# Latent attention: the row maxima written in rounded form, the rows of sums behind the last values, and in two of eight units the last low part behind the maxima

## The chip, the cores and the metric

The kernel runs on one core of one Trainium2 chip. Its time is the device time of one execution, in microseconds (us). The core has five engines: TensorE (PE in the profile; PEld are its weight loads), VectorE (DVE), ScalarE (ACT), GpSimd (POOL) and SyncE (SP), which issues most of the DMAs.

## What is computed

Two layers of a diffusion backbone for 128 context tokens and 1024 latent tokens. The change lies in layer 0, in the attention of the 1024 latent tokens over 128 cached and 1024 own keys, for 16 heads:

```python
s = (jnp.einsum('bqhd,bkhd->bhqk', q_nope, k_nope)
     + jnp.einsum('bqhr,bkr->bhqk', q_rope, k_rope)) * MLA_SCALE
p = softmax_f32(s).astype(v.dtype)
return jnp.einsum('bhqk,bkhd->bqhd', p, v)
...
return (o.reshape(b, n, MLA_WIDTH) * jax.nn.silu(gate)) @ w_out
```

A softmax may have any number taken off all scores of one query before the exponential, as long as it is the same number in the numerator and in the sum.

## The kernel before

Most products are made to keep float32's precision out of fp32r operands: a value is split into a rounded high part and a low part (the rest), and a product takes three passes, high by high, high by low, low by high. So each exponential of six of the nine key blocks is split: ACT writes the high part, DVE subtracts it for the low part.

The attention is a loop over 64 **units**: unit k is head k // 4 and query block k % 4 (256 queries). Nine blocks of 128 keys fill five PSUM banks (three named S, two named T) with transposed scores: keys on partitions, queries in columns. While unit k is worked on (`un`), the scores of the next one (`nx`) are made. The order of the steps on PE, ACT, DVE and POOL is written out by hand, in a table `ORDERS` with one row for each k % 8 (called the **kind** of a unit below). Each engine executes its instructions in that order and waits where an operand is not there. The steps that matter here:

- `s0`..`s4` (PE): scores of the next unit, a bank each. Bank S of `s0` is free again when `e0` of the present unit has read it.
- `m0`..`m4`: running maximum of the scores; `m0` a copy on ACT, the others on DVE.
- `e0`..`e4` (ACT): exponentials, a bank each. `h0`..`h2` (ACT) and `l0`..`l2` (DVE): their high and low parts.
- `+1`..`+4` (POOL): sums of the exponentials over the key blocks, five operations that each need the one before.
- `v68`, `v03`, `v45` (PE): values of key blocks 6 to 8 (six matmuls in the profile's groups), 0 to 3 (twelve) and 4 and 5 (six).
- **Sums**: `L0` (PE) turns the sums into columns, `L1` (DVE) reduces them to one number for each query and inverts it, `L2` and `L3` (DVE) split it into high and low part (`lir`), `L4` (PE) makes it a row again, `L5` (ACT) copies the row into `row`.
- **Maxima of the next unit**: `M0` (PE) turns them into columns, `M1` (DVE) reduces them (`nm`), `M2` and `M3` (DVE) split them (`nmr`), `M4` (PE) makes them a row, `M5` (ACT) copies the row into two rows of the queries' tile `q`, and `X` (PE, nine matmuls) adds them to all scores. Only then can the next unit's `e0` begin.
- `V` (ACT): the values out of PSUM (`ol`). `F` (PE, `finish`): the row of inverted sums on all partitions, and the last product of the values. `O` (DVE): the gating.
- The other letters (`P`, `p`, `A`, `ES`, `EV`, `H`, `T`, `w`) place work of the next heads: projections, rope, prompt attention, weight splits.

`L0`, `M0`, `M4` and `L4` write the same PSUM bank, `pm`. Steps that the diff's functions don't show:

```python
def columns_to_rows(r, ps):
    for k in range(2):
        nc.tensor.matmul(ps[:, k * P:(k + 1) * P], r[:, 2 * k:2 * k + 2], identR, start=True, stop=True)
def max_rows_out(un):
    S.copy(un["ql"][64:66, un["qs"]], un["pm"][0:2, 256:512])
def sum_row_out(un):
    S.copy(row[0:2, :], un["rs"][0:2, 0:256])
```

Of the kernel before, what the change touches and what calls it, by code (L numbers as in the profile page):

```python
# [11 lines left out]
F32 = mybir.dt.float32  # L12
F32R = mybir.dt.float32r
AF = mybir.ActivationFunctionType
ALU = mybir.AluOpType
AX = mybir.AxisListType
# [3 lines left out]
P = 128  # L20
# [7 lines left out]
H = 16  # L28
# [5 lines left out]
EPS = 1e-6  # L34
GW = 64
ORDERS = [
# [8 lines left out]
]  # L45
NPF = 5
WHOLE = 6
# [10 lines left out]
def hybrid_step(ctx: ExitStack, tc: tile.TileContext, i, o):  # L58
    nc = tc.nc
    V, S, G = nc.vector, nc.scalar, nc.gpsimd  # L60
# [705 lines left out]
    def max_cols(un, pm):  # L766
        un["pm"] = pm
        for k in range(2):
            nc.tensor.transpose(pm[:, k * P:(k + 1) * P], un["rm"][:, k * P:(k + 1) * P], ident)

    def max_reduce(un):
        un["nm"] = p2a.tile([P, 2], F32, tag="nm2", name="nm2", bufs=2)
        V.tensor_reduce(un["nm"], un["pm"][:, 0:256].rearrange("p (a b) -> p a b", a=2), AX.X, ALU.max, negate=True)

    def part_hi(un, src, name):
        un[name] = r = p2a.tile([P, 4], F32R, tag=name, name=name, bufs=2)
        V.tensor_copy(r[:, 0::2], un[src])

    def part_lo(un, src, name):
        r = un[name]  # L780
        V.tensor_tensor(r[:, 1::2], un[src], r[:, 0::2].bitcast(F32), ALU.subtract)
# [98 lines left out]
    def new_unit(h, u):  # L880
        hp = hps[h]
        return dict(h=h, qs=slice(u * 256, u * 256 + 256), qA=hp["qA"], qh=hp["q2"][0], ql=hp["q2"][1], wv=head_wv[h],
                    banks=[], pf=[], pT=[])


    p2a = es_a.enter_context(tc.tile_pool(name="p2a", bufs=1, side="right", reuse_waits="tile"))
    q2_, qA_ = [[p2a.tile([P, NTOK], F32R, name=f"q2{x}_{n}") for x in range(2)] for n in range(2)], [
        [p2a.tile([P, NTOK], F32R, name=f"qA{x}_0") for x in range(2)]]

    def no_max(q2):  # L890

        G.memset(q2[1][64:66, NLAT:NTOK].bitcast(F32), 0.0)
    for q2 in q2_:
        no_max(q2)
# [13 lines left out]
    f, un, nx = None, None, new_unit(0, 0)  # L908
    with tc.high_priority(offset=300):
        for b in range(5):  # L910
            scores(nx, b)
            run_max(nx, b)
        max_cols(nx, bank("W"))
        max_reduce(nx)
        part_hi(nx, "nm", "nmr")
        part_lo(nx, "nm", "nmr")
        max_rows(nx)
        max_rows_out(nx)
        last_scores(nx)
# [22 lines left out]
    def do(fn, x, *a):  # L942
        if x:
            fn(x, *a)
# [61 lines left out]
    for k, (h, u) in enumerate(units):  # L1006
        if k + 1 < len(units):

            hn, n = units[k + 1]
            do_rest((hn, (0, 1, 1, 2)[n]))  # L1010
        if u == 3 and h < H - 1 or (h, u) == (H - 1, 0):
            first, *rest = prompt_work(h)
            heads.appendleft(first)
            prompts.extend(rest)
            if h + 2 < H:
                heads.extend(head_work(h + 2))
        if u == 1 and h % 2 == 1 and h < H - 1:
            while prompts:
                do_rest(1)
        splits = deque()  # L1020
        if u == 1 and h + 1 < H:
            if h:
                splits.append(lambda: load_v(h + 1))
            splits.append(lambda: h + 2 < H and head_raw.update({h + 2: load_head(h + 2, new_raw(0))}))
        if u == 2 and h + 2 < H:
            splits.append(lambda: split_qk(h + 2, head_raw[h + 2][0]))
            splits.append(lambda: split_r(h + 2, head_raw[h + 2][1]))
        f, un, nx = un, nx, new_unit(*units[k + 1]) if k + 1 < len(units) else None
        pm = None
        if k == len(units) - 2:  # L1030
            early_load()
        last = k == len(units) - 1
        for step in ORDERS[k % 8].split():
            if last and step in ("h0", "L0"):
                early_product((0, 1) if step == "h0" else (2,))
                n = "h0 L0".split().index(step)
                early_split(2 * n, (q2_[(H - 2) % 3], qA_[(H - 1) % 2])[n])
                load_half(2 * n + 4, new_raw())
            c, n = step[0], int(step[1:] or 0) if step[1:].isdigit() else step[1:]
            if c == "e":  # L1040
                exp(un, n)
            elif c == "F":
                do(finish, f)
            elif c == "O":
                do(finish_out, f)
            elif c == "E":
                do_evac({"V": V, "S": S}[n])
            elif c == "h":
                hi(un, n)
            elif c == "l":  # L1050
                lo(un, n)
            elif c == "s":
                do(scores, nx, n)
            elif c == "m":
                do(run_max, nx, n)
            elif c in "Pp":
                do_prod(c == "p")
            elif c == "H":
                if splits:
                    splits.popleft()()  # L1060
            elif c == "w":
                if 36 <= k < 44:
                    load_wo0(k - 36)
            elif c == "+":
                sums(un, n)
            elif c == "v":
                n = step[1:]
                values(un, range(int(n[0]), int(n[-1]) + 1))
            elif c == "M":
                if n == 0:  # L1070
                    pm = pm if pm is not None else bank("M")
                    do(max_cols, nx, pm)
                elif n == 1:
                    do(max_reduce, nx)
                elif n == 2:
                    do(part_hi, nx, "nm", "nmr")
                elif n == 3:
                    do(part_lo, nx, "nm", "nmr")
                elif n == 4:
                    do(max_rows, nx)  # L1080
                elif n == 5:
                    do(max_rows_out, nx)
            elif c == "L":
                if n == 0:
                    pm = pm if pm is not None else bank("M")
                    sum_cols(un, pm)
                elif n == 1:
                    sum_inverse(un)
                elif n == 2:
                    part_hi(un, "li", "lir")  # L1090
                elif n == 3:
                    part_lo(un, "li", "lir")
                elif n == 4:
                    sum_rows(un)
                elif n == 5:
                    sum_row_out(un)
            elif c == "A":
                do_after(1)
            elif c == "T":
                settle()  # L1100
            elif c == "V":
                values_out(un)
            elif c == "X":
                do(last_scores, nx)
            else:
                assert False, step
# [48 lines left out]
    for t in range(NT):  # L1155
        ps = bank("S")[:, :256] if t else early["ps"]
        for q in range(4) if t else ():
            n = 4 * (t - 1) + q
# [109 lines left out]
    for t in range(NT):  # L1268
# [4 lines left out]
        for q in range(4):  # L1273
            n = 32 + 4 * t + q
# [510 lines left out]
    for k in range(-2, N):  # L1785
# [15 lines left out]
        if k >= 0 and (its[k]["cg"], its[k]["e"]) == (0, 0):  # L1801
            p = its[k]["p"]
# [5 lines left out]
        for step in NORDER.split():  # L1808
            c, n = step[0], step[1:]
# [159 lines left out]
```

## Time and profile before

| | |
|---|---|
| median of 3 runs | 2148.03 us (2146.34 to 2150.01) |
| the profiled execution | 2152.5 us, its span from first to last instruction 2150.7 us |
| busy: PE / DVE / ACT / POOL | 94% / 64% / 49% / 38% of the span |
| mean granted TensorE clock | 0.982 of full speed |

Busy shares are means over the whole program. The attention loop runs from about 354 to 1175 us of the span. A "unit" below is about 12 to 14 us long.

### The profile page before, as it was taken

What the parts mean: (1) busy time and instruction counts of PE and PEld (TensorE: products, weight loads), DVE (VectorE), ACT (ScalarE), POOL (GpSimd) and SP (SyncE); (2) the same over time, 40 slices, a digit from 0 to 9 for tenths busy, and PEclk for the clock granted to TensorE, in tenths of its full rate; (3) what the DMA queues carried; (4) which work ended last, traced back from release to release, by engine and by line L of the source; (5) the groups of instructions that cost most, each with busy time, mean ns of one, the idle gap of its engine ahead of it and who ended that gap; (6) DMA issues with size and microseconds to landing.
All of it is one profiled execution on the core that took longest, in us unless ns stands there. A gap on an engine that the chain in (4) does not pass through costs nothing. (4 is left out here: it accounts for less than half of the span.)

```text
span 2150.7 us, 36948 instructions
## 1 busy us (share of the span) xinstructions
PE 2027.4 (94%) x12894; PEld 1857.6 (86%) x12894; DVE 1371.6 (64%) x3032; ACT 1057.4 (49%) x2430; POOL 821.9 (38%) x820
## 2 busy tenths in 40 slices
PE   8899998899999999999998799989999999999898
PEld 3899997888888898888898788889889999999686
DVE  4723886667777777786776735542215788888743
ACT  5645115455555565555554533342215666667631
POOL 1411213566766667776764500010001333333300
PEclk9999999999999999999999999999999999999899
DMA  8212753112221213221212733325424655556753
GB/s 296 92 69 91 241 172 84 51 53 61 57 70 45 68 53 84 61 76 35 75 31 84 232 128 124 117 87 180 151 97 145 187 171 179 176 183 199 217 150 97
DMA packets 177230, 256.44 MB, mean 119 GB/s; under 512 B 20946, under 2 KB 142578, under 8 KB 177044
## 3 DMA queue, kind: packets, MB, share of 16 engines
q1 hardware_dynamic: 176780, 253.71, 38.2%
q8 instruction: 102, 1.67, 0.3%
q14 instruction: 84, 0.69, 0.1%
q10 hardware_dynamic: 136, 0.26, 0.0%
q0 software_dynamic: 128, 0.11, 0.0%
HBM read 182.58 MB, written 51.49 MB: 109 GB/s over the span
## 5 line engine op out<-in xcount | busy, mean ns | idle before, releaser
L826 POOL TENSOR_TENSOR sm<-sm,pf 128x512 f32<-128x512 f32 (+1 forms) x192 | 260.6, 1357 | 17.9 <-ACT pf L805 4.0
L815 DVE TENSOR_TENSOR pT<-pf,pT 128x512 fp32r<-128x512 f32 x192 | 231.2, 1212 | 40.5 <-ACT pT L810 40.2
L88 PE MATMUL ps_W<-h,w 128*128 128x384 f32 x1152 | 237.6, 345 | 0.4 <-DVE w L83 0.4
L747 PE MATMUL ps_S<-qA,cKT 128*128 128x256 f32 x1152 | 202.8, 296 | 4.1 <-ACT pf L805 3.9
L88 PEld LDWEIGHTS ps_W<-h,w 128*128 128x128 f32 x1152 | 197.9, 188 | 6.4 <-DVE w L83 0.8
L88 PE MATMUL ps_S<-hT,w_hi 128*128 128x384 f32 x720 | 193.0, 347 | 4.3 <-DVE hT L83 2.6
L747 PEld LDWEIGHTS ps_S<-qA,cKT 128*128 128x128 f32 x1152 | 171.8, 193 | 10.6 <-ACT pf L805 6.3
L88 PE MATMUL ps_M<-pT,cK 128*128 128x256 f32 x1152 | 168.1, 290 | 0.0
L1655 POOL TENSOR_SCALAR pf<-pf,li 128x512 f32<-128x512 f32 x128 | 91.2, 712 | 198.5 <-DVE li L1652 180.2
L88 PEld LDWEIGHTS ps_M<-pT,cK 128*128 128x128 f32 x1152 | 146.5, 190 | 0.0
L88 PEld LDWEIGHTS ps_S<-hT,w_hi 128*128 128x128 f32 x720 | 133.8, 193 | 6.1 <-DVE hT L83 3.3
L823 POOL TENSOR_TENSOR sm<-pf 128x512 f32<-128x512 f32 x64 | 86.6, 1354 | 115.4 <-ACT pf L805 114.9
L88 PE MATMUL ps_S<-wo,og 128*128 128x512 f32 x432 | 124.9, 397 | 0.0
L88 PE MATMUL ps_S<-hT,w_lo 128*128 128x384 f32 x360 | 123.9, 345 | 0.0
L521 ACT COPY qt<-ps_W 128x384 f32<-128x384 f32 (+1 forms) x104 | 46.6, 448 | 149.6 <-PE ps_W L88 136.3
L810 ACT CAST pT<-pf 128x512 fp32r<-128x512 f32 x192 | 118.9, 631 | 0.0
L1649 ACT ACTIVATE pf<-pf,nm 128x512 f32<-128x512 f32 x128 | 93.0, 726 | 34.5 <-DVE nm L1646 30.9
L747 PE MATMUL ps_S<-q,KR 128*128 128x256 f32 x384 | 109.1, 285 | 0.4 <-DMA q<-w_raw 0.4
L805 ACT ACTIVATE pf<-ps_S 128x512 f32<-128x512 f32 x192 | 108.0, 597 | 0.2 <-PE ps_S L798 0.2
L747 PE MATMUL ps_T<-qA,cKT 128*128 128x256 f32 x576 | 101.7, 292 | 0.0
L792 ACT CAST q<-ps_M 2x256 fp32r<-2x256 f32 x63 | 22.8, 361 | 160.2 <-PE ps_M L786 160.1
L83 DVE TENSOR_TENSOR og<-w_raw,og 128x512 fp32r<-128x512 f32 x56 | 54.6, 994 | 70.0 <-ACT og L149 69.9
(379 smaller groups left out, 5133.3 us busy)
## 6 DMA issues: line engine op xcount, KB each, us to landing
w_raw<-in_w_ada SPq DMA_DIRECT2D x48, 512.0 KB
w_raw<-og_d SPq DMA_DIRECT2D x41, 512.0 KB
vw<-vd SPq DMA_DIRECT2D x128, 128.0 KB
bias<-in_bias SPq DMA_DIRECT2D x64, 192.0 KB
q<-rp SPq DMA_DIRECT2D x126, 96.0 KB
gate_d<-gt SPq DMA_DIRECT2D x48, 192.0 KB
w_raw<-in_wgate SPq DMA_DIRECT2D x16, 512.0 KB
gt<-gate_d SPq DMA_DIRECT2D x64, 128.0 KB
```

Source lines behind the costliest of these rows:

```text
L83: eng.tensor_tensor(out, a, b, ALU.subtract)
L88: nc.tensor.matmul(ps, lhs[a], rhs[b], start=first and n == 0, stop=last and n == 2)
L521: (eng.copy if eng is S else eng.tensor_copy)(out, src)
L747: nc.tensor.matmul(ps[:, c:c + 256], k_[:, j, :], q_[:, un["qs"]], start=c == 0 and n == 0, stop=n == 3, skip_group_check=True)
L792: S.copy(un["ql"][64:66, un["qs"]], un["pm"][0:2, 256:512])
L805: S.activation(pf, un["banks"][b][:, :w], AF.Exp)
L810: S.copy(un["pT"][b][0][:, :pf.shape[1]], pf)
L815: V.tensor_tensor(x[1], pf, x[0].bitcast(F32), ALU.subtract)
L823: G.tensor_tensor(un["sm"], un["pf"][0], pf, ALU.add)
L826: G.tensor_tensor(sm[:, :w], sm[:, :w], pf, ALU.add)
L1649: S.activation(it["pf", rg], it["pf", rg], AF.Exp, bias=it["nm", rg], scale=1.0, accum_out=it["li", rg])
L1655: G.tensor_scalar(it["pf", rg], it["pf", rg], it["li", rg][:, 0:1], 1.0, ALU.mult, ALU.mult)
```

## The change

Three things. The maxima are written by `M1` in rounded form (fp32r) at once, into one of two tiles of four columns whose low columns were set to zero at the start, so `M2` and `M3` are gone: every score of a query is lowered by the rounded maximum. In all eight rows of the table `L4` and `L5` stand behind `v45`, and `M4`, `M5` right before it. In the rows of kinds 5 and 6 `l2` stands behind `m4`. The diff, with two of the eight table rows:

```diff
-    "F e0 H O ES s0 H e1 +1 h0 s1 l0 T e2 A m0 e3 m1 e4 s2 P m2 T h1 +2 +3 s3 l1 h2 l2 m3 P +4 p s4 m4 v68 ES p L0 M0 L1 M1 L2 v03 p A M2 L3 ES M3 w L4 M4 v45 A M5 L5 X V",
+    "F e0 H O ES s0 H e1 +1 h0 s1 l0 T e2 A m0 e3 m1 e4 s2 P m2 T h1 +2 +3 s3 l1 h2 m3 P +4 p s4 m4 l2 v68 ES p L0 M0 L1 M1 L2 v03 p A L3 ES w M4 M5 v45 L4 L5 A X V",
-    "H F e0 H e1 s0 T O +1 h0 s1 l0 e2 A m0 m1 h1 e3 s2 +2 P P +3 s3 l1 m2 h2 l2 e4 ES m3 v68 s4 +4 A m4 p L0 M0 L1 P M1 A A L2 M2 A v03 P L3 M3 ES L4 A M4 w v45 M5 X L5 V ES",
+    "H F e0 H e1 s0 T O +1 h0 s1 l0 e2 A m0 m1 h1 e3 s2 +2 P P +3 s3 l1 m2 h2 l2 e4 ES m3 v68 s4 +4 A m4 p L0 M0 L1 P M1 A A L2 A v03 P L3 ES A M4 M5 w v45 L4 L5 X V ES",
...
     def max_reduce(un):
-        un["nm"] = p2a.tile([P, 2], F32, tag="nm2", name="nm2", bufs=2)
-        V.tensor_reduce(un["nm"], un["pm"][:, 0:256].rearrange("p (a b) -> p a b", a=2), AX.X, ALU.max, negate=True)
+        un["nmr"] = nmr_[un["h"] * 4 + un["qs"].start // 256 & 1]
+        V.tensor_reduce(un["nmr"][:, 0::2], un["pm"][:, 0:256].rearrange("p (a b) -> p a b", a=2), AX.X, ALU.max,
+                        negate=True)
...
+    nmr_ = [p2a.tile([P, 4], F32R, name=f"nmr{x}") for x in range(2)]
+    for x in nmr_:
+        G.memset(x.bitcast(F32), 0.0)
...
         max_reduce(nx)
-        part_hi(nx, "nm", "nmr")
-        part_lo(nx, "nm", "nmr")
...
-                elif n == 2:
-                    do(part_hi, nx, "nm", "nmr")
-                elif n == 3:
-                    do(part_lo, nx, "nm", "nmr")
```

What this makes of the engines' order is shown at three places. First PE at the end of unit 28 (kind 4), as in most units: the last matmuls of `v03`, the rows, `v45` (six matmuls `ps_M<-pT`), and `X` (`ps_S<-q,KR`). Before:

```order
L88 MATMUL ps_M<-pT_8090,cK_864 128x256
L786 MATMUL ps_M<-identR,lir 2x128 x2
L786 MATMUL ps_M<-identR,nmr 2x128 x2
L88 MATMUL ps_M<-pT_8095,cK_863 128x256
L88 MATMUL ps_M<-pT_8096,cK_863 128x256
L88 MATMUL ps_M<-pT_8095,cK_864 128x256
L88 MATMUL ps_M<-pT_8095,cK_863 128x256
L88 MATMUL ps_M<-pT_8096,cK_863 128x256
L88 MATMUL ps_M<-pT_8095,cK_864 128x256
L798 MATMUL ps_S<-q_1_2873,KR_867 128x256 x6
```

and with the change:

```order
L88 MATMUL ps_M<-pT_7978,cK_864 128x256
L788 MATMUL ps_M<-identR,nmr_2877 2x128 x2
L88 MATMUL ps_M<-pT_7983,cK_863 128x256
L88 MATMUL ps_M<-pT_7984,cK_863 128x256
L88 MATMUL ps_M<-pT_7983,cK_864 128x256
L88 MATMUL ps_M<-pT_7983,cK_863 128x256
L88 MATMUL ps_M<-pT_7984,cK_863 128x256
L88 MATMUL ps_M<-pT_7983,cK_864 128x256
L788 MATMUL ps_M<-identR,lir 2x128 x2
L800 MATMUL ps_S<-q_1_2873,KR_867 128x256 x6
```

The row of sums (`lir`) moved from ahead of the row of maxima (`nmr`) to between `v45` and `X`; nothing else on PE moved. Second, ACT at the same place, with the engines whose semaphores each row waits for: `M5`, `L5`, `V` and the next unit's first two exponentials. Before:

```order
L792 CAST q_1_2873<-ps_M 2x256 [waits DVE_49,PE_49]
L860 CAST row<-ps_M 2x256
L843 COPY ol<-ps_M 128x256 [waits PE_49]
L805 ACTIVATE pf<-ps_S 128x512 [waits PE_49,Pool_49]
L805 ACTIVATE pf<-ps_S 128x512 [waits PE_49]
```

and with the change:

```order
L794 CAST q_1_2873<-ps_M 2x256 [waits DVE_49,PE_49]
L862 CAST row<-ps_M 2x256 [waits PE_49]
L845 COPY ol<-ps_M 128x256
L807 ACTIVATE pf<-ps_S 128x512 [waits PE_49,Pool_49]
L807 ACTIVATE pf<-ps_S 128x512 [waits PE_49]
```

The order is the same, but the copy of the row of sums now has a wait of its own for PE, and the three rows behind it stand in its queue. On PE the first matmul of `L4` waits for ACT as well as for DVE now (`L788 MATMUL ps_M<-identR,lir 2x128 [waits DVE_49,Activation_49]`), since `M5` reads the same bank. Third, DVE in unit 29 (kind 5), from the second and third running maximum on: `l1`, `l2`, `m3` (two rows), `m4`, then `L1`, `M1`, `L2`, `M2`, `L3`, `M3`. Before:

```order
L760 TENSOR_TENSOR rm<-ps_S,rm 128x512 x2
L815 TENSOR_TENSOR pT_8299<-pf,pT_8298 128x512
L815 TENSOR_TENSOR pT_8315<-pf,pT_8314 128x512
L760 TENSOR_TENSOR rm<-ps_T,rm 128x512
L762 TENSOR_TENSOR rm<-rm 128x256
L764 TENSOR_TENSOR rm<-ps_T,rm 128x256
L853 TENSOR_REDUCE li_8351<-ps_M 128x2
L854 RECIPROCAL li_8351<-li_8351 128x2
L773 TENSOR_REDUCE nm_8354<-ps_M 128x2
L777 CAST lir<-li_8351 128x2
L777 CAST nmr<-nm_8354 128x2
L781 TENSOR_TENSOR lir<-li_8351,lir 128x2
```

and with the change:

```order
L760 TENSOR_TENSOR rm<-ps_S,rm 128x512 x2
L817 TENSOR_TENSOR pT_8183<-pf,pT_8182 128x512
L760 TENSOR_TENSOR rm<-ps_T,rm 128x512
L762 TENSOR_TENSOR rm<-rm 128x256
L764 TENSOR_TENSOR rm<-ps_T,rm 128x256
L817 TENSOR_TENSOR pT_8199<-pf,pT_8198 128x512
L855 TENSOR_REDUCE li_8235<-ps_M 128x2
L856 RECIPROCAL li_8235<-li_8235 128x2
L774 TENSOR_REDUCE nmr_2876<-ps_M 128x2
L779 CAST lir<-li_8235 128x2
L783 TENSOR_TENSOR lir<-li_8235,lir 128x2
```

The low part `l2` moved from ahead of the last three maxima to behind them, and the two rows on `nmr` are gone. On POOL only two small memsets at the start are new; the DMA queue's order is the same but for one load of a gate in two places.

## Rows read from the trace of the kernel before

**Rows 1.** The page: busy time, share of the span and instructions.
```profile
PE 2027.4 (94%) x12894; PEld 1857.6 (86%) x12894; DVE 1371.6 (64%) x3032; ACT 1057.4 (49%) x2430; POOL 821.9 (38%) x820
```
**Rows 2.** Who waited for whom, 354 to 1175 us: us, times, longest.
```profile
PE ps_M L769 <- DVE rm L764: 29.3, 31, 1.8
...
PE ps_M L786 <- DVE lir L781: 10.9, 17, 1.9
```
**Rows 3.** Groups by line, DVE, 340 to 1175 us: count, busy us, mean ns.
```profile
L777 DVE CAST nmr<-nm 128x2 fp32r<-128x2 f32 x64 | 11.3, 177 | 0.0
```
**Rows 4.** Timeline of PE, end of unit 28: start us, us, instruction.
```profile
722.15 0.28 PE L786 MATMUL ps_M<-identR,lir 128*2 128x128 f32 x2
722.27 0.28 PE L786 MATMUL ps_M<-identR,nmr 128*2 128x128 f32 x2
...
723.16 0.87 PE L798 MATMUL ps_S<-q,KR 66*128 66x256 f32 x6
...
724.58 0.70 PE L747 MATMUL ps_S<-qA,cKT 128*128 128x256 f32 x3
```
**Rows 5.** Timeline of ACT, the same stretch: M5, L5, V, e0 with e1.
```profile
722.59 0.36 ACT L792 CAST q<-ps_M 2x256 fp32r<-2x256 f32 x1 [1.79 <-PE ps_M L786]
722.97 0.36 ACT L860 CAST row<-ps_M 2x256 fp32r<-2x256 f32 x1
723.35 0.37 ACT L843 COPY ol<-ps_M 128x256 f32<-128x256 f32 x1
723.65 1.08 ACT L805 ACTIVATE pf<-ps_S 128x512 f32<-128x512 f32 x2
```
**Rows 6.** Timeline of POOL in unit 24 (kind 0): the first of the sums.
```profile
663.53 1.30 POOL L823 TENSOR_TENSOR sm<-pf 128x512 f32<-128x512 f32 x1 [1.35 <-ACT pf L805]
```
**Rows 7.** Timeline of PE in unit 24: L0, v03, L4 (in brackets the idle time before).
```profile
670.49 0.44 PE L849 MATMUL ps_M<-ident,sm 128*128 128x128 f32 x2 [0.17 <-POOL sm L826]
...
670.91 1.68 PE L88 MATMUL ps_M<-pT,cK 128*128 128x256 f32 x12
672.46 0.28 PE L786 MATMUL ps_M<-identR,lir 128*2 128x128 f32 x2
```
**Rows 8.** Timeline of PE, unit 25 (kind 1) and into 26: L4, then s0.
```profile
684.64 0.28 PE L786 MATMUL ps_M<-identR,lir 128*2 128x128 f32 x2 [0.36 <-DVE lir L781]
...
687.18 0.62 PE L747 MATMUL ps_S<-qA,cKT 128*128 128x256 f32 x3 [0.31 <-ACT pf L805]
```
**Rows 9.** Timeline of PE, unit 27 (kind 3): L4.
```profile
710.14 0.28 PE L786 MATMUL ps_M<-identR,lir 128*2 128x128 f32 x2 [0.55 <-DVE lir L781]
```
**Rows 10.** Timeline of PE, units 29 and 30 (kinds 5 and 6): M0 and M4.
```profile
734.09 0.44 PE L769 MATMUL ps_M<-ident,rm 128*128 128x128 f32 x2 [1.27 <-DVE rm L764]
...
735.96 0.29 PE L786 MATMUL ps_M<-identR,nmr 128*2 128x128 f32 x2
...
748.07 0.44 PE L769 MATMUL ps_M<-ident,rm 128*128 128x128 f32 x2 [1.78 <-DVE rm L764]
...
750.16 0.28 PE L786 MATMUL ps_M<-identR,nmr 128*2 128x128 f32 x2
```
**Rows 11.** Timeline of DVE, units 29 to 31: l2, M1; l1, l2; l2.
```profile
731.14 1.21 DVE L815 TENSOR_TENSOR pT<-pf,pT 128x512 fp32r<-128x512 f32 x1
...
735.10 0.40 DVE L773 TENSOR_REDUCE nm<-ps_M 128x2 f32<-128x256 f32 x1
...
743.54 1.74 DVE L815 TENSOR_TENSOR pT<-pf,pT 128x512 fp32r<-128x512 f32 x1
...
745.20 1.22 DVE L815 TENSOR_TENSOR pT<-pf,pT 128x512 fp32r<-128x512 f32 x1
...
758.36 0.68 DVE L815 TENSOR_TENSOR pT<-pf,pT 128x512 fp32r<-128x512 f32 x1
```
**Rows 12.** Timeline of POOL in unit 30 (kind 6): a low part of projected queries.
```profile
747.30 1.04 POOL L83 TENSOR_TENSOR qA<-qt,qA 128x384 fp32r<-128x384 f32 x1 [0.28 <-ACT qA L149]
```
**Rows 13.** One window: PE, PEld, DVE, ACT, POOL busy, granted PE clock.
```profile
410.30:417.20 6.90, 6.90 (x32) 6.72 (x32) 2.36 (x4) 4.78 (x12) 4.20 (x4) 0.51 0.44 110
```

12 rows, old and new, of the table ORDERS are left out of this document.

## Prediction

> **What bounds the kernel now.** I read the page first: PE is busy for 94% of the span [rows 1], so only what keeps PE waiting, or slow, has a price. Then the waits inside the attention loop. The largest there is `M0`'s on the running maximum on DVE, 29.3 us in 31 waits; `L4`'s on the low part of the inverted sums is 10.9 us in 17, the longest 1.9 [rows 2]. Both are latencies of a chain that ends on DVE while PE has nothing else in its order. The timelines say which units they belong to: `M0` waits 1.27 us in unit 29 and 1.78 us in unit 30 [rows 10], kinds 5 and 6, and `L4` waits 0.36 us in kind 1 and 0.55 us in kind 3 [rows 8, 9]. Last, a window: after unit 4's long wait TensorE ran 6.9 us at half its clock (0.51, the 1.2 GHz level) [rows 13].
>
> The listed waits are a little short. The twelve matmuls of `v03` are modelled 1.68 us long, but `L4` begins 1.55 us after their start when nothing holds it [rows 7]. So about 0.13 us is to be added to each wait of `L4`.
>
> **The two operations that go.** `M2` and `M3` are about 0.18 us each on DVE, 64 times [rows 3], some 23 us of DVE together. In the loop they stand behind `M1`, where DVE soon waits for PE again, so they shorten only the way from `M1` to `M4`. Nearly all that is worth is inside the next terms, since `M4` had to wait behind `L4` anyway. Only before the loop does the chain run alone: twice 0.18 us, **-0.4 us**. The two memsets on POOL lie under the first projections: nothing, and two small operations if they don't.
>
> **`L4` behind `v45`: what it gives.** `M4` no longer stands behind `lir`, and `M1` comes before `L2` and `L3`. In kind 1 that is worth 0.36 + 0.13 = 0.49 us, in kind 3 0.55 + 0.13 = 0.68 us a unit.
>
> **What it costs: the exponentials start later.** Take the hand-over at the end of unit 28. Before, the matmuls of `L4` began at 722.15, of `M4` at 722.27, `X` at 723.16, and the next `s0` at 724.58 [rows 4]. On ACT `M5` began 0.32 us after `M4`, then came `L5` (722.97), `V` (723.35) and `e0` (723.65) [rows 5], so `e0` began 0.49 us after `X`. Now `L4` goes into PE's queue one 0.12 us step ahead of `X`, so `L5` can't begin before 0.32 us behind that, 0.20 us after `X`; before, it began 0.19 us ahead of `X`. `V` and `e0` stand behind it on ACT and follow by 0.38 and 0.30 us, as in the rows: `e0` at 0.88 us after `X`, **0.39 us later**. PE's own sequence is as long as before. `L4`'s new wait for `M5` costs nothing here: `M5` ends 0.68 us after `M4`'s start, `L4`'s turn comes at 0.89 - 0.12 = 0.77 us.
>
> Who feels the 0.39 us? `s0` could start 1.42 us after `X` [rows 4]; `e0`, about 0.6 us long (two in 1.08), now ends at 1.48, so `s0` loses up to 0.1 us everywhere. More is lost where something hangs on the exponentials without slack:
> - Kind 0: POOL's five sums start when the second exponential is there (663.53, after a wait for ACT), and `L0`, 7 us later, waits 0.17 us for them [rows 6, 7]. +0.39 us.
> - Kind 1: the same chain. +0.39 - 0.49 = -0.10 us.
> - Kind 2: `s0` already waits 0.31 us for `e0` at 687.18 [rows 8]. +0.39 us.
> - Kind 3: `L0` waits for nothing in the timeline, so part of the delay is hidden. I set +0.22, a little over half; with -0.68 that is -0.46 us.
> - Kinds 4 and 7 show no such wait; I set +0.1 us for the two together, the loss of `s0`.
>
> **`l2` behind `m4`.** In kinds 5 and 6 DVE works without a break from `l0` to `m4`, so `M0` comes earlier by `l2`: 1.21 and 1.22 us [rows 11], less 0.08 us by which the records of neighbours overlap (743.54 + 1.74 against 745.20), 1.13 and 1.14 us. Of that the later exponentials, through `h0` and `l0`, take back 0.3 and 0.39 us. `l2` then stands between `m4` and `L1`. Its price is not shown there: 0.68 us where it ran alone, 1.2 us under POOL's sums, and its sister `l1` took 1.74 us [rows 11]. I take 1.0, near the middle of the first two, since POOL's sums are over by then but another POOL operation is near.
> - Unit 29: `M0` at 734.09 - 1.13 + 0.3 = 733.26. `l2` starts with it and ends at 734.26. From `M0`'s end (734.53) to `M1`'s (735.50) it was 0.97 us, so `M1` ends at 735.23. `M4` was at 735.96 [rows 10], so it comes 0.73 us earlier; 0.12 us of `L4` now stand behind it: **-0.61 us**.
> - Unit 30: `M0` comes 1.14 - 0.39 = 0.75 us earlier, 747.32; `l2` until 748.32, `M1`'s end 749.29. `M4`'s turn is at 750.16 - 0.75 - 0.12 = 749.29 as well: nothing is lost again, **-0.75 us**.
>
> So of `M0`'s 3 us half is gained.
>
> The Trainium skill weighs `l2` otherwise ("SBUF — State Buffer", section "SBUF: two separate sides"): VectorE operations with two SBUF inputs and GpSimd operations share a port pair as an exclusive lock, and whoever comes first holds it for its whole instruction. The spread from 0.68 to 1.74 us agrees with a shared port. By it `l2` at 747.3 meets POOL's operation at 747.30 [rows 12]: ahead of it, it would run its 0.68 us, and the sum would be some 3 us better; just behind it, it is a rival below.
>
> **Sum.** Eight units: 0.39 - 0.10 + 0.39 - 0.46 + 0.10 - 0.61 - 0.75 = -1.04 us. Units 8 to 63 are seven such rounds: -7.3 us. Units 0 to 7 differ, since a head's rope work stands between `L2` and `L3`: there is `L4`'s longest wait, 1.9 us [rows 2], in unit 4. It moves behind `v45` (0.77 us) rather than going, and `e0` waits with it; I set -2 us for the round. The clock: 6.9 us at half speed cost 3.4 us [rows 13]. They follow the wait that shrinks, so I take them as gone, -3.4 us. With the start: -0.4 - 7.3 - 2.0 - 3.4 = **-13.1 us**, 2152.5 to 2139.4 us for the profiled execution. The runs' median is 4.5 us lower, 2148.0, so **2134.9 us**, 0.61% less.
>
> Bounds of this case. If `l2` costs 1.74 us (14 x 0.74 = 10 us) and the clock gives nothing, 2134.9 + 10.4 + 3.4 = 2149. If `l2` costs 0.68 us (14 x 0.32, -4.5) and the first round gives 2 us more, 2128.
>
> **Rivals.**
> - *The later exponentials cost nothing.* For it: ACT waits 1.79 us before `M5` [rows 5], so it catches up within the unit. Against: `s0` and POOL's chain wait at their start, before ACT can catch up. Then the round is -0.49 - 0.68 - 0.61 - 0.75 and 0.69 us more in kinds 5 and 6, -3.2 us; seven are 15 us more than above: 2120 us. 15%.
> - *`l2` is caught behind POOL.* If it begins only when POOL's 1.04 us operation ends, `L1` and `M4` come that much later in 14 units: +14.6 us, the gain is gone: 2149 us. For it: in unit 30 the two start together [rows 12]; against: no operation of DVE in the rows waits so long. 13%.
> - *Slower: ACT is late at `M5`.* `L5` needs `L4`, which needs `M5`, and ACT has projections to evacuate ahead of it. If this holds `e0` 0.4 us longer in all kinds, 56 x 0.4 = 22 us: 2157 us. It turns the sign from 0.23 us on (13.1 / 56). Against: ACT stands idle 1.79 us ahead of `M5` [rows 5]. 10%.
> - *It does nothing that can be measured.* Waits of `M0` become waits of `M4` in full (1.4 us a round, 9.5 us), and the half clock stays: 2148 us. 10%.
>
> **How the numbers follow.** The forecast has 52%. A measurement of this kernel tells 0.2% (4.3 us) from no change. The forecast's own range is 2128 to 2149, and its upper end, where two bounds meet, is the unlikely one. The range to hold 8 in 10 runs from 2118, just past the first rival, to 2150, which takes in the second and the fourth. Faster: 52 + 15, and 6 of the second and fourth, 73%; same 18%; slower 9%.
>
> **What would show it.** Right: `L4`'s wait on DVE gone from the list in steady units, `M0`'s 29.3 us down by more than half, a new wait of `M4` on `M1` of about 0.2 us in kind 5, `e0` 0.88 us after `X`, and `L0`'s wait for POOL in kind 0 up from 0.17 to about 0.55 us. Wrong: `e0` back at 0.5 us after `X` (the first rival), `l2` of 1.7 us and more, or starting late, behind `m4` (the second), or `M5` late and `X` waiting for it (the third).

## The result, and the profile after

The changed kernel takes 2127.43 us (median of 4 runs, 2124.26 to 2128.94) against 2149.02 us of the kernel before in the same comparison: 0.9889 of it, 95% interval 0.9872 to 0.9906. A second comparison gave 0.9867 (0.9844 to 0.9890). It is faster by 1.1 to 1.3%, 22 to 28 us. The forecast was 2134.9 us, 0.61% less, in a range of 2118 to 2150: the sign and the range hold, and the gain is about twice the forecast.

The profiled execution has a span of 2126.5 us, 24.2 us less than before. The page, its first part (as [rows 1]):

```profile
PE 2021.3 (95%) x12894; PEld 1856.7 (87%) x12894; DVE 1358.8 (64%) x2904; ACT 1045.9 (49%) x2430; POOL 824.4 (39%) x822
```

DVE has 128 instructions less (2904 against 3032) and 12.8 us less of busy time; `M2` and `M3` were some 23 us. No other instruction came or went, so some 10 us are single operations that got longer; one of them will be seen. The waits of PE in the attention loop, 350 to 1146 us (as [rows 2]: us in total, times, longest):

```profile
PE ps_M L769 <- DVE rm L764: 15.6, 27, 1.0
PE ps_M L851 <- POOL sm L828: 12.4, 21, 1.7
PE ps_S L747 <- ACT pf L807: 5.6, 8, 1.6
PE ps_M L788 <- DVE lir L783: 1.3, 2, 0.8
```

`M0`'s wait for the running maximum fell from 29.3 to 15.6 us, `L4`'s for the sums from 10.9 us in 17 waits to 1.3 us in 2. `M4`'s wait for `M1`, which the forecast expected in kind 5, isn't there. What the change pays stands in the two middle rows: `L0` waits for POOL's sums, `s0` for the exponentials. Before, in the window of [rows 2], these were

```profile
PE ps_M L849 <- POOL sm L826: 7.7, 13, 1.6
PE ps_S L747 <- ACT pf L805: 3.9, 8, 1.4
```

`L0`'s wait is no clean sign of the later exponentials, though: with the move of `l2` alone (`b_l2` below), which leaves `e0` where it was, it is 10.7 us in 18 waits.

**Where the 24.2 us came from.** The trace can be cut at the first matmul of the first `X` and at that of the last. Ahead of the loop the kernel took 344.5 us before and 340.9 us after, in the loop 818.0 and 793.3 us, behind it 988.2 and 992.3 us. So the loop gives 24.6 us, and the rest gives 3.7 and loses 4.1. Neither of those belongs to the change: in the second profile of the same changed kernel they are 345.3 and 989.2 us, and over all kernels below 339 to 345 and 986 to 992 us. The forecast's 0.4 us at the start can't be seen in that.

Part of the loop's gain is TensorE's clock. Besides the 6.9 us of [rows 13] three shorter stretches of the loop before held a part at half clock. The windows, with the granted clock as the third number from the end:

```profile
444.00:447.90 3.90, 3.72 (x16) 3.54 (x17) 1.30 (x4) 3.25 (x8) 1.81 (x2) 0.56 0.62 160
...
837.00:840.40 3.40, 3.18 (x16) 3.10 (x17) 2.14 (x11) 0.00 (x0) 0.78 (x2) 0.50 0.28 82
...
1150.50:1155.50 5.00, 5.00 (x29) 5.00 (x30) 3.32 (x6) 3.79 (x8) 4.23 (x4) 0.66 0.79 254
```

Each row's time times what its clock lacks to 1 is 1.7 us, three times, and 3.4 us for [rows 13]: 8.5 us. Both kernels also run at half clock where the loop begins, and the cut at the first `X` falls differently there: the part behind it is 4.4 us before and 6.8 us after. From there on, the loop after ran at the full clock. The part before, the part after, and the rest after:

```profile
344.50:348.90 4.40, 4.35 (x20) 4.35 (x21) 1.30 (x1) 3.69 (x6) 3.10 (x5) 0.50 0.49 112
...
341.40:348.20 6.80, 6.22 (x30) 5.93 (x29) 2.38 (x3) 5.71 (x10) 5.44 (x6) 0.50 0.47 108
...
348.30:1134.20 785.90, 749.71 (x5642) 708.25 (x5640) 585.33 (x1052) 437.08 (x1020) 545.99 (x468) 1.00 0.22 60
```

So the loop lost 8.5 + 2.2 = 10.7 us to the clock before and 3.4 us after. The second profile of the changed kernel has a loop of 795.4 us with two more stretches at half clock (at 426 and 1129 us), 6.5 us lost in all. So the clock is worth 4 to 7 us of the loop's gain of 22.5 and 24.6, and the waits the rest, 17 or 18 us.

**By kinds.** From one `X` to the next, units 24 to 31, where no half clock lies (us, from the start of `X`'s first matmul):

| kind | 0 | 1 | 2 | 3 | 4 | 5 | 6 | 7 | sum |
|---|---|---|---|---|---|---|---|---|---|
| before | 11.68 | 12.16 | 13.07 | 12.43 | 12.01 | 13.69 | 14.20 | 12.68 | 101.92 |
| after | 11.78 | 11.83 | 13.26 | 11.81 | 11.90 | 13.33 | 12.94 | 12.67 | 99.51 |
| difference | +0.10 | -0.33 | +0.19 | -0.62 | -0.11 | -0.36 | -1.26 | -0.01 | -2.41 |
| forecast | +0.39 | -0.10 | +0.39 | -0.46 | +0.1 with 7 | -0.61 | -0.75 | | -1.04 |

Every sign is as forecast but that of kinds 4 and 7, which the forecast took together, and every unit but that of kind 5 is cheaper than its term.

**The hand-over.** PE at the end of unit 28 (start, us, instruction; as [rows 4]): `M4`, `L4`, `X`, `s0`.

```profile
706.55 0.28 PE L788 MATMUL ps_M<-identR,nmr 128*2 128x128 f32 x2
...
707.44 0.28 PE L788 MATMUL ps_M<-identR,lir 128*2 128x128 f32 x2
707.56 0.92 PE L800 MATMUL ps_S<-q,KR 66*128 66x256 f32 x6
...
709.03 0.71 PE L747 MATMUL ps_S<-qA,cKT 128*128 128x256 f32 x3
```

And ACT (as [rows 5]): `M5`, `L5`, `V`, `e0` with `e1`.

```profile
706.87 0.36 ACT L794 CAST q<-ps_M 2x256 fp32r<-2x256 f32 x1 [1.46 <-PE ps_M L788]
707.76 0.36 ACT L862 CAST row<-ps_M 2x256 fp32r<-2x256 f32 x1 [0.53 <-PE ps_M L788]
708.03 0.36 ACT L845 COPY ol<-ps_M 128x256 f32<-128x256 f32 x1
708.29 1.06 ACT L807 ACTIVATE pf<-ps_S 128x512 f32<-128x512 f32 x2
```

`L5` begins 0.20 us after `X`, as forecast, but `V` follows it by 0.27 us, not 0.38, and `e0` that by 0.26 us, not 0.30. So `e0` begins 0.73 us after `X` (708.29 - 707.56): 0.24 us later than before, not 0.39. Who pays for that: in unit 24 `L0` waits 0.27 us for POOL (0.17 before), and into unit 26 `s0` waits 0.50 us for `e0` (0.31 before).

```profile
655.84 0.44 PE L851 MATMUL ps_M<-ident,sm 128*128 128x128 f32 x2 [0.27 <-POOL sm L828]
...
672.38 0.61 PE L747 MATMUL ps_S<-qA,cKT 128*128 128x256 f32 x3 [0.50 <-ACT pf L807]
```

**Kinds 5 and 6.** `M0` in units 29 and 30 (as [rows 10]), still with a wait, 0.86 and 0.48 us instead of 1.27 and 1.78:

```profile
718.17 0.44 PE L769 MATMUL ps_M<-ident,rm 128*128 128x128 f32 x2 [0.86 <-DVE rm L764]
...
730.89 0.44 PE L769 MATMUL ps_M<-ident,rm 128*128 128x128 f32 x2 [0.48 <-DVE rm L764]
```

DVE there: the fold of `m3` (L762), `m4` and `l2` of unit 29, and the fold and `l2` of unit 30.

```profile
716.37 1.22 DVE L762 TENSOR_TENSOR rm<-rm 128x256 f32<-128x256 f32 x1
717.69 0.42 DVE L764 TENSOR_TENSOR rm<-ps_T,rm 128x256 f32<-128x256 f32 x1
718.03 0.68 DVE L817 TENSOR_TENSOR pT<-pf,pT 128x512 fp32r<-128x512 f32 x1
...
729.88 0.42 DVE L762 TENSOR_TENSOR rm<-rm 128x256 f32<-128x256 f32 x1
...
730.75 0.69 DVE L817 TENSOR_TENSOR pT<-pf,pT 128x512 fp32r<-128x512 f32 x1
```

And POOL's low part of the queries in both units:

```profile
716.29 1.01 POOL L83 TENSOR_TENSOR qA<-qt,qA 128x384 fp32r<-128x384 f32 x1
...
731.41 1.02 POOL L83 TENSOR_TENSOR qA<-qt,qA 128x384 fp32r<-128x384 f32 x1 [0.53 <-ACT qA L149]
```

`l2` behind `m4` takes 0.68 us, its price alone [rows 11], in both units. POOL's operation starts in unit 30 when `l2` is nearly through. In unit 29 it starts 0.08 us ahead of the fold, and there the fold takes 1.22 us instead of 0.42 us. So POOL did hold DVE up, but at another operation than the forecast had watched.

### The profile page after: what moved, and what is told of

The parts are those of the page before. It is cut to its first block, busy times and chain, and to the rows that moved or that the text cites. A ratio compares the mean times of both kernels' runs of the same rounds, so it can differ in the third digit from the quotient of the medians.

```text
span 2126.5 us, 36852 instructions
## 1 busy us (share of the span) xinstructions
PE 2021.3 (95%) x12894; PEld 1856.7 (87%) x12894; DVE 1358.8 (64%) x2904; ACT 1045.9 (49%) x2430; POOL 824.4 (39%) x822
## 5 line engine op out<-in xcount | busy, mean ns | idle before, releaser
L88 PE MATMUL ps_W<-h,w 128*128 128x384 f32 x1152 | 240.2, 348 | 0.4 <-DVE w L83 0.4
L88 PEld LDWEIGHTS ps_W<-h,w 128*128 128x128 f32 x1152 | 200.5, 191 | 6.4 <-DVE w L83 0.8
L88 PE MATMUL ps_S<-hT,w_hi 128*128 128x384 f32 x720 | 190.1, 342 | 4.3 <-DVE hT L83 2.6
L88 PE MATMUL ps_M<-pT,cK 128*128 128x256 f32 x1152 | 164.2, 289 | 0.0
L88 PEld LDWEIGHTS ps_M<-pT,cK 128*128 128x128 f32 x1152 | 146.0, 189 | 0.0
L88 PEld LDWEIGHTS ps_S<-hT,w_hi 128*128 128x128 f32 x720 | 131.3, 189 | 6.4 <-DVE hT L83 3.3
L88 PE MATMUL ps_S<-wo,og 128*128 128x512 f32 x432 | 124.9, 397 | 0.0
L88 PE MATMUL ps_S<-hT,w_lo 128*128 128x384 f32 x360 | 122.4, 341 | 0.0
L838 PE MATMUL ps_M<-pf,cKf 128*128 128x256 f32 x384 | 93.4, 379 | 0.0
```

Source lines behind the costliest of these rows:

```text
L88: nc.tensor.matmul(ps, lhs[a], rhs[b], start=first and n == 0, stop=last and n == 2)
L838: nc.tensor.matmul(un["pso"], cKf[:, j - WHOLE, :], un["pf"][j // 2][:, c], start=j == WHOLE, stop=False)
```

## The experiments

The theory after the two traces: the rounding pays only with the late `L4`, and the late `L4` only with the rounding; `l2`'s move pays by itself; a late `e0` has a price in every unit; POOL holds the fold in kind 5. The rivals: rounding alone, or `L4`'s place alone, gives the gain; `e0` costs nothing.

**b_round**: the kernel before with the rounded maxima alone (the change's `max_reduce`, and in every row of the table the edit shown).

```diff
-    "... L0 M0 L1 M1 L2 M2 v03 A L3 L4 M3 M4 v45 M5 L5 V X w",
+    "... L0 M0 L1 M1 L2 v03 A L3 L4 M4 v45 M5 L5 V X w",
```

> The kernel before with the rounded maxima alone: M2 and M3 are gone, every other step stands where it stood. Theory (the two operations stood in the chain of small DVE operations that releases L4 and M4, and that chain ends last in almost every unit): L3 ends about 0.1 us earlier in each of 64 units, M4 still stands behind L4, so about 6 us less, 2143 us. Rival (they were hidden behind v03, as the prediction had it): 2148 to 2149 us, the start's 0.4 us apart.

Measured: 0.9992 of before (0.9977 to 1.0006), no change that the times resolve (in the trace the loop is 1.7 us shorter, and `L4` still waits 10.4 us in 16 waits); the rival, which is what the prediction had said, holds. Why, DVE shows in unit 25 (kind 1). Before: `L2`, `M2`, `L3`, `M3`.

```profile
683.74 0.65 DVE L777 CAST lir<-li 128x2 fp32r<-128x2 f32 x1
684.30 0.15 DVE L777 CAST nmr<-nm 128x2 fp32r<-128x2 f32 x1
684.42 0.16 DVE L781 TENSOR_TENSOR lir<-li,lir 128x2 fp32r<-128x2 f32 x1
```

With the rounding alone: `L2`, `L3`.

```profile
680.85 0.52 DVE L779 CAST lir<-li 128x2 fp32r<-128x2 f32 x1
681.40 0.16 DVE L783 TENSOR_TENSOR lir<-li,lir 128x2 fp32r<-128x2 f32 x1
```

`L3` begins 0.03 us after `L2`'s end in both (684.42 - 684.39, 681.40 - 681.37). It needs `L2`'s result and waits for it; `M2` only filled that wait.

**b_l4**: the kernel before with `L4` and `L5` behind `v45`, `M2` and `M3` kept.

```diff
-    "... L0 M0 L1 M1 L2 M2 v03 A L3 L4 M3 M4 v45 M5 L5 V X w",
+    "... L0 M0 L1 M1 L2 v03 A M2 L3 M3 M4 M5 v45 L4 L5 V X w",
```

> The kernel before with L4 and L5 behind v45 and M4, M5 ahead of it, but M2 and M3 kept and l2 where it was. Theory: M4 then waits for M3, which ends where it ended before, so M4 doesn't come earlier, X comes 0.12 us later (L4 now between), and e0 0.24 us after that: 0.2 us in 64 units, about 13 us slower, 2162 us. Rival (the place of L4 is the gain, rounding only tidies up): 0.5 to 0.7 us less in kinds 1 and 3, some 8 us faster, 2141 us.

Measured: 1.0052 of before (1.0032 to 1.0073), slower, as the theory had it; the loop grew by 7.5 us although the half clock cost 2.5 us less. PE's waits, 355 to 1180 us:

```profile
PE ps_M L769 <- DVE rm L764: 27.1, 29, 2.1
PE ps_M L786 <- DVE nmr L781: 11.4, 23, 2.0
PE ps_M L849 <- POOL sm L826: 9.3, 17, 1.4
```

The 10.9 us of `L4` waiting for `lir` became 11.4 us of `M4` waiting for `M3`'s `nmr`: the same chain of small operations, another customer. What remains of the move is its cost.

**b_l2**: the kernel before with `l2` behind `m4` in kinds 5 and 6 alone.

```diff
-    "... s3 l1 h2 l2 m3 P +4 p s4 m4 v68 ...",
+    "... s3 l1 h2 m3 P +4 p s4 m4 l2 v68 ...",
```

> The kernel before with l2 behind m4 in kinds 5 and 6 alone. Theory (the l2 move is worth its own duration in kind 6 and about 0.4 us in kind 5, whatever L4 does): 1.6 us a round, 13 us in eight, and 2 to 8 us of half clock behind M0's long waits that goes with it: 2128 to 2134 us. Rival (the parts need each other: with L4 in front of M4 the wait only moves to L4): 2143 to 2149 us.

Measured: 0.9931 (0.9913 to 0.9950), 14.6 us less in the loop. Units 29 and 30 are 0.45 and 1.15 us shorter and no other of that round changes by more than 0.03 us; some 4 us of the 14.6 are clock. In the time it is 13.5 us less (2138.05 against 2151.59), a little short of the theory's 13 us and 2 to 8 us of clock; unit 4's stretch of half clock stayed. The rival falls.

**a_l2back**: the changed kernel with `l2` back in front of `m3` in kinds 5 and 6.

```diff
-    "... s3 l1 h2 m3 P +4 p s4 m4 l2 v68 ...",
+    "... s3 l1 h2 l2 m3 P +4 p s4 m4 v68 ...",
```

> The changed kernel with l2 back in front of m3 in kinds 5 and 6 (rounded maxima and the late L4 stay). Theory: the round loses 1.6 us again, 13 us, and up to 8 us of half clock come back: 2140 to 2148 us. Rival (the rounded maxima and L4 carry the gain): within 4 us of the changed kernel, 2127 to 2131 us.

Measured: 0.9949 (0.9931 to 0.9967), 2142.87 us, as the theory had it: 8.7 us of the gain are left, and the rival falls. So rounding and `L4` together are worth 0.5%, `l2` alone 0.7%, and all three 1.1 to 1.3%: the two halves add.

**a_vfirst**: the changed kernel with `V` ahead of `L5`.

```diff
-    "... M4 M5 v45 L4 L5 V X w",
+    "... M4 M5 v45 L4 V L5 X w",
```

> The changed kernel with V ahead of L5 on ACT in all eight rows, nothing else. V needs v45 alone, which ends 0.12 us before L4, so V starts 0.08 us after X, L5 0.35 us, and e0 0.61 instead of 0.73 us after X. Theory (the late exponentials are what the change pays): half of the 0.24 us comes back, some 0.1 us in kinds 0, 1 and 2 and less elsewhere, 3 to 5 us in all, 2122 to 2125 us. Rival (they cost nothing): within 1.5 us of the changed kernel.

Measured: 0.9864 (0.9847 to 0.9881), 2121.34 us. ACT at the end of unit 28, where `X` begins at 707.53:

```profile
706.84 0.36 ACT L794 CAST q<-ps_M 2x256 fp32r<-2x256 f32 x1 [1.46 <-PE ps_M L788]
707.61 0.37 ACT L845 COPY ol<-ps_M 128x256 f32<-128x256 f32 x1 [0.41 <-PE ps_M L88]
707.88 0.36 ACT L862 CAST row<-ps_M 2x256 fp32r<-2x256 f32 x1
708.14 1.06 ACT L807 ACTIVATE pf<-ps_S 128x512 f32<-128x512 f32 x2
```

`e0` at 0.61 us after `X`, as computed, and `V` waits 0.41 us for `v45` (L88), though no copy stands between `M5` and it. It begins 0.77 us after `M5`, and in the kernel before, where `L5` stood between, 0.76 us (723.35 against 722.59, [rows 5]). The loop is 5.3 us shorter than in the changed kernel; in units 24 to 31 those of kinds 0, 2 and 7 are 0.10 to 0.13 us shorter, kind 3 0.06 us, the others the same. Not all of it is `e0`: two waits of `F` for `V`, 1.1 us in units 6 and 7, which the change had brought, are gone as well.

**a_row2**: the changed kernel with `L5` made twice.

```diff
     def sum_row_out(un):
         S.copy(row[0:2, :], un["rs"][0:2, 0:256])
+        S.copy(row[0:2, :], un["rs"][0:2, 0:256])
```

> The changed kernel with the copy L5 made twice, the second the same as the first, so that V and e0 come 0.27 us later in every unit. Theory (a late e0 is paid in full in kinds 0, 1, 2 and 5, where POOL's sums, the next scores or the running maximum end last, and in part in the others): 1.2 to 1.8 us a round, 10 to 14 us slower than the changed kernel, 2137 to 2141 us. Rival (ACT catches up within the unit, so that a late e0 is hidden): within 3 us of it.

Measured: 0.9976 (0.9966 to 0.9987), 2145.54 us, 18 us slower than the changed kernel. ACT at the end of unit 28, `X` at 719.35:

```profile
719.55 0.36 ACT L862 CAST row<-ps_M 2x256 fp32r<-2x256 f32 x1 [0.53 <-PE ps_M L788]
719.95 0.36 ACT L863 CAST row<-ps_M 2x256 fp32r<-2x256 f32 x1
720.22 0.36 ACT L845 COPY ol<-ps_M 128x256 f32<-128x256 f32 x1
720.48 1.06 ACT L807 ACTIVATE pf<-ps_S 128x512 f32<-128x512 f32 x2
```

The second copy begins only when the first has ended, so `e0` came 1.13 us after `X`, 0.40 us later than in the changed kernel, and the edit was larger than meant. The eight units take 101.91 instead of 99.51 us: 2.4 us for 0.40, where `a_vfirst` got 0.42 us back for 0.12 (99.09 us). Kinds 0 to 4 and 7 each lost 0.31 to 0.42 us, kind 6 0.10 us, kind 5 nothing (the theory had it among those that pay in full). So a late `e0` is paid in six of eight units; ACT does not catch up in time.

**a_fold**: the changed kernel with `m4` ahead of the fold.

```diff
-        if b == 3:
-            V.tensor_tensor(m, m, rm[:, 256:512], ALU.max)
         if b == 4:
             V.tensor_tensor(m, ps[:, 0:256], m, ALU.max)
+            V.tensor_tensor(m, m, rm[:, 256:512], ALU.max)
```

> The changed kernel with the maximum of the last block (m4, which reads PSUM) ahead of the fold of the two halves in SBUF. In unit 29 (kind 5) the fold took 1.22 us instead of 0.42 us, beside POOL's low part of the queries. Theory (the fold is held by POOL's operation, and that is why kind 5 gained 0.4 instead of 0.6 us or more): m4 is done meanwhile, M0 comes 0.4 to 0.5 us earlier in kind 5, and nothing changes elsewhere: 3 to 4 us less, 2123 us. Rival (the fold's own length, or m4's wait, sets M0): no change, 2127 us.

Measured: 0.9864 (0.9849 to 0.9879), 2121.05 us. In unit 29 `m4` (now L762) and then the fold (L763) on DVE, beside POOL, and `M0` on PE:

```profile
712.31 0.42 DVE L762 TENSOR_TENSOR rm<-ps_T,rm 128x256 f32<-128x256 f32 x1
712.77 0.69 DVE L763 TENSOR_TENSOR rm<-rm 128x256 f32<-128x256 f32 x1
...
712.16 1.02 POOL L83 TENSOR_TENSOR qA<-qt,qA 128x384 fp32r<-128x384 f32 x1
...
713.51 0.44 PE L768 MATMUL ps_M<-ident,rm 128*128 128x128 f32 x2 [0.34 <-DVE rm L763]
```

`m4`, which reads PSUM, runs its 0.42 us beside POOL. The fold ends 0.28 us after POOL's operation (713.46 and 713.18), and so it did in the changed kernel (717.59 and 717.30), though it began 0.08 us into POOL's operation there and 0.6 us into it here. `M0`'s wait falls from 0.86 to 0.34 us, and unit 29 takes 12.80 instead of 13.33 us. "Nothing changes elsewhere" was wrong: in kinds 0 and 1 most units are 0.18 us shorter, and kind 2 went 0.4 us down in four units and 0.5 us up in the other four. In unit 24 it is POOL that is held: its last sum takes 0.97 us in the changed kernel, where the fold (654.78) just precedes it, and 0.73 us here, and `L0` waits for that sum.

```profile
654.78 0.42 DVE L762 TENSOR_TENSOR rm<-rm 128x256 f32<-128x256 f32 x1
...
654.82 0.97 POOL L828 TENSOR_TENSOR sm<-sm,pf 128x256 f32<-128x256 f32 x1
```

```profile
651.51 0.73 POOL L827 TENSOR_TENSOR sm<-sm,pf 128x256 f32<-128x256 f32 x1
```

**a_l2_27**: the changed kernel with `l2` behind `m4` in kinds 2 and 7 too (the same edit as in kinds 5 and 6).

> The changed kernel with l2 behind m4 in kinds 2 and 7 as well, where M0 waits 0.45 and 0.68 us for DVE. Theory (what made l2's move pay in kinds 5 and 6 holds wherever M0 waits behind l2): both waits go, 0.9 to 1.1 us a round, 7 to 9 us less, 2119 us. Rival (behind m4 the operation meets POOL's, or holds L1 and M1 so that M4 waits for them): half of that or nothing, 2123 to 2128 us.

Measured: 0.9858 (0.9844 to 0.9872), 2120.75 us, as the theory had it, the gain a little under its 7 to 9 us. Unit 26 takes 12.59 instead of 13.26 us and unit 31 12.26 instead of 12.67, the other six are the same within 0.02 us: 1.1 us a round.

**after_again, c_v_l2, c_all**: the changed kernel once more; with `a_vfirst` and `a_l2_27` in one; with `a_fold` as well.

> The changed kernel itself, on one chip with the two combinations, as their base. Theory and rival alike: 0.988 to 0.990 of the kernel before, 2126 to 2129 us; its stretches before and behind the attention loop may differ by 2 to 4 us from the first profile, as they did between the other kernels, its loop by less than 1 us.

> The changed kernel with V ahead of L5 in all rows, and l2 behind m4 in kinds 2 and 7 as well. Theory (two causes on different engines, each with its price, so that the gains add): 5.4 + 6.7 us less than the changed kernel, 2115 us, 0.983 to 0.985 of before. Rival (both shorten the way from one unit's X to the next one's M4, so that the second gain is partly the first again): 2119 to 2121 us.

> As the one above, and m4 ahead of the fold in SBUF. Theory (the fold is held by POOL only in kind 5 and partly in others): another 3 to 5 us, 2110 to 2112 us, 0.981 to 0.983. Rival (with l2 now behind m4 in kinds 2 and 7 too, the later fold meets POOL there, as it cost 0.5 us in four units of kind 2): no better than without it, 2115 us.

Measured, on one chip: 0.9867 (0.9844 to 0.9890), 0.9825 (0.9807 to 0.9844) and 0.9808 (0.9790 to 0.9826), or 2126.38, 2115.60 and 2112.07 us. The loop of the changed kernel was 795.4 us here and 793.3 us in the first profile: further apart than the 1 us expected; the half clock cost it 3.1 us more here. The first two gains add (783.0 us of loop; 793.3 - 5.3 - 5.1 would be 782.9). With the fold the loop is 781.2 us, 1.8 us less where 4.2 us were won alone: in units 24 to 31 those of kinds 0, 1 and 5 are 0.18, 0.18 and 0.51 us shorter, but that of kind 2 is 0.34 us longer, as the rival had it. All four runs with the fold are shorter than all four without (2113.72 us at most against 2114.69 at least), but the intervals against the kernel before overlap: that the fold still pays there is likely, not shown.

## Why the prediction was right, and where its sizes were off

**The two operations that go**: nothing in the loop; right within what the times resolve (`b_round`). But the text gave the rounding too small a part in the rest. "`M4` had to wait behind `L4` anyway" is true of the old order; with `L4` gone from there `M4` waits for `M3` in full (`b_l4`). The rounding is what turns a loss of 0.5% into a gain of 0.5%.

**`L4` behind `v45`**: 0.49 and 0.68 us in kinds 1 and 3 were right as sizes of the wait. What made them was not the chain's own length, as the prediction had it, but POOL: `L2` took 0.65 and 0.70 us in units 25 and 27 against a usual 0.16 (last section). Missing was that the chain ended last in kinds 4 and 7 as well, without a wait that the list shows: from `M0` to `M4` unit 28 took 1.95 us before (720.32 to 722.27) and 1.66 us after, 0.12 us of it `L4`, so that 0.17 us was waiting in a unit without one in the list. In unit 31 it is 0.20 us, in the units of kinds 0, 2, 5 and 6 some 0.05. Kind 4 gains by that, and its exponentials come no later (next point).

**The later exponentials**: the step that failed. "`V` and `e0` stand behind it on ACT and follow by 0.38 and 0.30 us, as in the rows" took the distance from `L5` to `V` in [rows 5] for ACT's own pace. It was `V`'s wait for `v45`: the row has no bracket, since `L5`'s record covers that time, but `V` starts as long after `M5` with no `L5` between (`a_vfirst`). The kernel before had such a place itself, at the end of unit 27: the row of kind 3 had `V` ahead of `L5`, and there `V` waits for `v45` in plain sight.

```profile
711.35 0.37 ACT L843 COPY ol<-ps_M 128x256 f32<-128x256 f32 x1 [0.41 <-PE ps_M L88]
711.62 0.36 ACT L860 CAST row<-ps_M 2x256 fp32r<-2x256 f32 x1
```

ACT's own pace is 0.27 us, and 0.24 instead of 0.39 us was lost. In kind 4 nothing was: its `e0`, behind those two copies, began 0.73 us after `X` before the change, and does so after. With the hidden waits of the point before, kinds 0 to 4 and 7 gave -0.78 us a round where the forecast had +0.32; this is 1.1 of the 1.4 us by which the round was off. That the price is real, the first rival's question, is shown both ways (`a_row2`, `a_vfirst`), though not in every unit.

**`l2` behind `m4`**: -1.36 us a round forecast for kinds 5 and 6 together, -1.62 measured, by a different split. In kind 6 `l2` took 0.68 us instead of the 1.0 assumed, and the later exponentials took nothing back: `l0` began 0.2 us later after `X` and ended 0.09 us earlier, in the two traces 0.54 and 0.55 us after an operation of POOL that ran beside it, so that POOL and not `e0` set its end. In kind 5 the fold met POOL and kept 0.8 of the 1.2 us. The Trainium skill ("SBUF — State Buffer", section "SBUF: two separate sides") has it that GpSimd and a VectorE operation with two SBUF inputs share a port pair as an exclusive lock, held by the first for its whole instruction. That had the better price here: what the prediction drew from it, 0.68 us ahead of POOL's operation, is what the trace of unit 30 shows, though the two meet there for only 0.03 us (731.41 to 731.44), so that this unit is no test of the rule. `a_fold` agrees with it: the held fold ends 0.28 or 0.29 us after POOL's operation, whenever it began. So do the low parts of [rows 11]: those of 1.21, 1.22 and 1.74 us each ended 0.55 us after the operation of POOL that was running when they began. The spread was not a price of `l2` with a middle to take, but the time at which POOL was done.

**The first round**: -2 us forecast; units 0 to 7 lost 6.8 us, of which 3.9 are clock, so 2.9.

**The clock**: 3.4 us forecast for one stretch, 4 to 7 measured in the loop. That the half clock went with the shorter waits is likely but not shown stretch by stretch: `b_l2`, which leaves unit 4's wait, kept the stretch at 408 to 416 us, and the changed kernel itself had two others in its second profile. Some of this gain may be chance.

**Rivals**: the second happened to another operation, at 0.8 us in kind 5 alone. The third did not happen: ACT waits 1.46 us ahead of `M5` in the changed kernel too. The fourth falls with the measured time.

**The signs**: of the five that the prediction named for being right, only the first came as stated, `L4`'s waits on DVE (17 before, 2 after). `M0`'s fell by 47%, not by more than half; the wait of `M4` on `M1` did not come; `e0` came at 0.73 us, not 0.88; and `L0`'s wait in kind 0 rose to 0.27 us, not 0.55. The range held because it was wide, 32 us: the rounds behind the first, -7.3 us in the sum, gave -17.8 us, of which 3.4 are clock.

## What to carry to other kernels

When several operations feed one queue, ask of each which of its results the next customer really needs: here the same move of `L4` lost 0.5% with the low part of the maxima in the chain and gained 0.5% without. A distance between two rows of one engine is its own pace only if the second waited for nothing else, and a wait that lies under the record before it has no bracket; look for a second place where the row stands without the first. And work that nobody waits for yet belongs behind the operation that is waited for, in every row of a table where that wait is listed: kinds 2 and 7 had it as well.

## What the runs showed of the hardware

A small operation can be held as long as a large one: `L2`, a cast of 128x2 values, took 0.65 and 0.52 us in the rows of `b_round` above, against a usual 0.16, and both times ended 0.02 or 0.03 us after this operation of POOL (in the kernel before, and with the rounding alone):

```profile
683.36 1.01 POOL L83 TENSOR_TENSOR qA<-qt,qA 128x384 fp32r<-128x384 f32 x1 [1.23 <-ACT qA L149]
```

```profile
680.32 1.02 POOL L83 TENSOR_TENSOR qA<-qt,qA 128x384 fp32r<-128x384 f32 x1 [1.09 <-ACT qA L149]
```

`L4`'s wait of 0.36 us in unit 25 [rows 8] is of that size: `L3` and then `L4` stand behind this cast. It is no single case: in the kernel before 14 of the 64 casts `L2` took more than 0.25 us, and every one ended 0.02 or 0.03 us after an operation of POOL that had begun before it.

When a held operation ends can be read from POOL's rows. Of the 192 low parts `l0` to `l2` of the kernel before, the two that began while no operation of POOL ran took 0.68 us. 180 took more than 0.75 us, and 179 of these ended 0.54 to 0.56 us after the operation of POOL that was running when they began. The fold ends 0.28 us after it, the small cast 0.02 us. Each is 0.13 or 0.14 us less than the operation takes alone (0.68, 0.42 and 0.16 us).

An operation that reads PSUM was not held: 46 of the 64 `m4` of the kernel before ran beside POOL and took 0.41 to 0.43 us, as the 18 others did.
